# A hybrid decoder layer: order-only dependencies for the transfers of the first pair, and one mask with a difference of values

## The chip, the cores and the metric

The kernel runs on one core of a Trainium2 chip. The core has five engines that run side by side, each through its own instructions in order: TensorE (PE; its weight loads are listed as PEld), VectorE (DVE), ScalarE (ACT), GpSimd (POOL) and SyncE (SP). An instruction waits on semaphores where it needs another engine's result, and whatever stands behind it on its engine waits too. SP does no arithmetic here: it starts nearly all transfers between the chip's main memory and the on-chip memory, in the order of its queue. ACT and POOL start some as well. The metric is the device time of one execution in microseconds (us), lower is better. A profile is one execution recorded by the hardware profiler, and its own time stands beside the span from its first to its last instruction.

## The reference

The layer works on 2048 tokens of width 1024 in float32. In short:

```python
hn = rms_norm(h, mix_pre_g)
proj = hn @ w_in                       # q (8 heads of 64), k and v (2 heads), and the input of a GLU
s = q.k / 8 + bias[distance]           # each query sees itself and the 127 tokens before it
p = softmax over s and a learned sink per head
attn_out = p @ v
conv_out = silu(layer_norm(depthwise_conv31(glu) + b)) @ w_conv_pw
mixed = concatenate([attn_out, conv_out]) @ w_out
h = h + rms_norm(mixed, mix_post_g)
hn = rms_norm(h, ffn_pre_g)
ff = (silu(hn @ w_gate) * (hn @ w_up)) @ w_down      # inner width 2816
h = h + rms_norm(ff, ffn_post_g)
```

In the attention, queries are taken in blocks of 128. A block of queries sees the keys of its own block up to its own position, and those of the block before from the next position on. So for a query at place q and a key place k in the block, exactly one of the two keys counts: the current one for k <= q, the one before for k > q.

## The kernel before

The 2048 tokens are four tiles of 512 (t = 0 to 3), the feature dimensions blocks of 128. A matmul of float32 values is done as three matmuls of split values (a rounded high part, and the rest as low part), which is what `three` and `product` do; ACT makes the high parts and DVE or POOL the low parts (`split_w`, `split_f`, `lo`).

The stages have letters, which stand behind the @ in the names of the profile: A is the input projection (`stage_a`, one per tile), B the attention (`stage_b`), C the convolution, done as 31 multiply-adds per channel block on DVE (`stage_taps`, written to `y_scr`) and a tail (`stage_tail`), W the output projection with its norms (`stage_w`, `norm_w`), H the operands of the feed-forward part, F its first product with the gate and up weights, G its second with the down weights. F and G treat two tiles of tokens at once, the first pair (tiles 0 and 1, labels F0, G0) and the second (tiles 2 and 3, labels F2, G2), by Strassen's scheme with seven block products in place of eight. Some of the first products are made earlier (`stage_pre`), kept in `keeps` and loaded again (`fetch`) when the seven-product stage (`stage_p1`) needs them. `stage_p1` reads two tiles of weights per matrix (`loads`, lines 951 to 959), makes four sums of them on DVE (`sums`), splits them, multiplies, and stores the results in `mids`. `stage_tsums` (L1065) makes the sums of the down weights meanwhile and stores them in `td`. `stage_p2` loads blocks of `mids` (tiles `fa`) and of down weights or their sums (tiles `mb`) three steps ahead (`load`, L1117).

The order of the work is set by two things. The code runs one main stage and, beside it, several lanes (`Lane`), each of which is given turns by a hand-set rate: attention, convolution taps, convolution tails, output projections and operands of the feed-forward part are lanes. From that program order a scheduler makes the order of every engine's instructions with a timeline of its own: among the instructions that are ready on its timeline it takes the earliest in program order. An instruction can so be moved ahead of others that are not ready. `tied(r)` (L113) gives `r` an order-only dependency on the last matmul of the main stage, `lead_pe`: the scheduler does not place `r` before that matmul, but no semaphore and no wait on the chip comes from it. Before the change, `tied` is used for a few transfers (L1051, L1054, L1072). `defer(n, emit)` hands an instruction out n steps later in program order.

In the attention, `front(b)` makes the scores of a block of queries. The scores with the block before and with the current block are merged into one 128 x 128 square by the mask `upper` (L456), so only 128 columns go through the softmax. `back(b)` turns the probabilities on TensorE, ACT copies them out (L497), and POOL makes two masked copies of each group of four heads, one for the current block and one for the block before (L499). The matmuls (L517) add both products in one bank, with values from `vtok`, which holds the tile's four blocks of 128 tokens and the last block of the tile before (L414, L415). In the first block of all there is no block before.

The norms take a sum of squares of 1024 columns on ACT into a tile `junk` that nobody reads (L272, L738, L760).

The on-chip tiles come from rings with a tag and a fixed number of buffers, and a tile waits for the release of the one that had its buffer.

Of the kernel before, what the change touches and what calls it, by code (L numbers as in the profile page):

```python
# [23 lines left out]
D = 1024  # L24
# [13 lines left out]
def layer_kernel(ctx, tc, x, xT, cols, rows, sinks, relb, onehot, w_in, w_pw, w_out, w_gate, w_up, w_down, out):  # L38
# [28 lines left out]
    def sm(n, dt=F32):  # L67
        kind = "A" if lab[0][0] == "G" else lab[0][0]
        return sb.tile([P, 8], dt, tag="sm" + kind, name=nm("sm"), bufs=16)[:, 0:n]
# [49 lines left out]

    def defer(n, emit):  # L120
        later.append([n, emit])
# [91 lines left out]
    ones = cst.tile([P, 1], F32, name="ones")  # L213
# [19 lines left out]
    neg = cst.tile([P, 1], F32, name="neg")  # L233
# [8 lines left out]
    junk = cst.tile([P, D], BF16, name="junk")  # L242
    vtok = cst.tile([P, 5, P], F32, name="vtok")
# [83 lines left out]
    def stage_a(t, hn, before_kv, hooks, post=None):  # L327
# [79 lines left out]
        for i in range(4):  # L407
            oq = proj(10 + i)
            if i == 0:
                pv = mm()  # L410
                for s in range(4):
                    nc.tensor.transpose(pv[:, s * P : (s + 1) * P], vt[:, s * P : (s + 1) * P], ident)
                if t:
                    nc.vector.tensor_copy(vtok[:, 0], vtok[:, 4])  # L414
                nc.vector.tensor_copy(vtok[:, 1:5].rearrange("p a b -> p (a b)"), pv)  # L415
# [14 lines left out]
    def stage_b(t):  # L430
# [54 lines left out]
        def back(b):  # L485
# [3 lines left out]
            for g in range(2):  # L489
# [8 lines left out]
                for kb in range(1 if first else 0, 2):  # L498
                    nc.gpsimd.affine_select(  # L499
                        out=pg[:, kb].rearrange("p (i q) -> p i q", q=P),  # L500
                        in_=pg[:, 1].rearrange("p (i q) -> p i q", q=P),
                        compare_op=ALU.is_ge if kb else ALU.is_gt,
                        fill=0.0,
                        base=0,
                        pattern=[[0, 4], [1 if kb else -1, P]],
                        channel_multiplier=-1 if kb else 1,
                    )
# [51 lines left out]
    def stage_taps(t):  # L559
        L = f"C{t}"  # L560
        for c in range(4):
# [8 lines left out]
            nc.sync.dma_start(y_scr[c, :, t * T : (t + 1) * T], y)  # L570
# [62 lines left out]
    def stage_x():  # L633
        lab[0] = "X0"
        rel = cst.tile([32, 8], F32, name="rel")
# [96 lines left out]
    def norm_w(w, spill, acc, mtag):  # L732
# [3 lines left out]
        ssq = sm(4)  # L736
        for s in range(4):
            act(junk, acc[s], AF.Square, accum_out=ssq[:, s : s + 1])  # L738
            yield 0.5
            lab[0] = L  # L740
        r = rsqrt(ssq, 4, D, w < 3)
        yield 3
        lab[0] = L
        ssq2 = sm(4)
        for s in range(4):
# [14 lines left out]
            act(junk, acc[s], AF.Square, accum_out=ssq2[:, s : s + 1])  # L760
            yield 1.5
        lab[0] = L
        r2 = rsqrt(ssq2, 4, D, w < 3)
# [178 lines left out]
    def stage_p1(ws, ops, mid, keep):  # L942
# [8 lines left out]
        def loads(m):  # L951
            if m < len(MATS):
# [3 lines left out]
                nc.sync.dma_start(r0, src[2 * pr].rearrange("p (a b) -> p a b", a=2))  # L956
                r1 = t_("chl", (P, 2, T))
                nc.sync.dma_start(r1, src[2 * pr + 1].rearrange("p (a b) -> p a b", a=2))
# [38 lines left out]
        for q, (m, j, i, nst) in enumerate(todo):  # L997
# [10 lines left out]
            if j == 0:  # L1008
                bk = {}
                if not gate:  # L1010
                    blocks = {}
                    if pre:
                        blocks[3] = f2("fa")
                        nc.sync.dma_start(blocks[3], mid[0, pr])
# [17 lines left out]
            else:  # L1032
# [7 lines left out]
                else:  # L1040
# [3 lines left out]
                    if i in (3, 4, 6):  # L1044
# [20 lines left out]
    def stage_tsums(td):  # L1065
        L = "G0"
        for pr in range(NF // 2):
# [6 lines left out]
            b11, b12, b21, b22 = b  # L1074
            for to, o, p_, q_ in ((0, b11, b12, b11), (2, b12, b22, b12), (1, b22, b22, b11), (3, b21, b21, b22)):
                lab[0] = L
                vtt(o, p_, q_, ALU.subtract)
                nc.sync.dma_start(td[to, pr], o)
                yield 1

    def finish(L, gb, jobs, pool=True):
# [3 lines left out]
        for j, (rows_, halves) in enumerate(jobs):  # L1085
            for n in range(2):
                act(junk[:, 0:T], halves[n], AF.Square, scale=D**-0.5, accum_out=ssq[:, 2 * n + j : 2 * n + j + 1])
# [5 lines left out]
        for j, (rows_, halves) in enumerate(jobs):  # L1093
            ht = f4("wx" if L == "G0" else "mid")
            nc.sync.dma_start(ht, h_scr[rows_])
            for n in range(2):
                cs = slice(n * T, (n + 1) * T)
                stt(halves[n], halves[n], r[:, j : j + 1], ht[:, cs], ALU.mult, ALU.add)
                nc.sync.dma_start(out[rows_, cs], halves[n])
            yield 2.0  # L1100
            lab[0] = L

    def stage_p2(ws, am, td, last=False):
# [13 lines left out]
        def load(i):  # L1117
            if i < len(steps):
# [45 lines left out]
        def scale_even(h):  # L1164
            for b in (2 * h, 2 * h + 1):
                lab[0] = L
                c = home("c11", "x", b)
                act(junk[:, 0:T], c, AF.Square, scale=D**-0.5, accum_out=sse[:, b : b + 1])
# [69 lines left out]
        for b in range(4):  # L1238
# [4 lines left out]
            act(junk[:, 0:T], banks[b], AF.Square, scale=D**-0.5, accum_out=ssq)  # L1243
# [246 lines left out]
```

## Time and profile before

| what | value |
|---|---|
| time, median of 3 runs | 2036.23 us (2028.73 to 2038.02) |
| time of the profiled execution | 2033.91 us |
| its span | 2032.2 us |
| mean granted clock of TensorE | 0.987 |
| busy: TensorE, DVE, ACT, POOL | 1959.0, 1504.8, 988.8, 382.4 us |
| moved by transfers | 451.44 MB, 222 GB/s in the mean |
| attention masks on POOL (L499) | 62, from 129 to 592 us |
| seven-product stage of the first pair | about 686 to 1033 us |
| second product of the first pair | about 1033 to 1380 us |

In lines of the profile the form is "line engine operation out<-in", with the tile names of the program without numbers; a tile's letter behind the @ is its stage. `x62` counts instructions. In an answer about waits, "PE tr@B L108 <- POOL p@B L499: 10.4, 4, 6.8" says that TensorE stood idle before matmuls of L108 into tile `tr` of stage B, that the semaphore which came last was POOL's for L499, and that this took 10.4 us in 4 waits, the longest 6.8. In a timeline the first number is the start in us, the second the duration, and square brackets hold the idle time of the engine before it and what ended it. In rows of stretches "A:B length, ..." the busy times of PE, PEld, DVE, ACT and POOL follow with the number of instructions in brackets, then the granted clock of TensorE as a share of full speed, the share of time that the transfer engines were busy, and GB/s. Rows of one tile or line give the shortest, the median and the longest duration in ns.

### The profile page before, as it was taken

The numbers are of one execution on the slowest core, as the hardware profiler recorded it, in microseconds if no ns is written. First come the engines' busy times: TensorE is split into PE (matmuls) and PEld (weight loads), VectorE is DVE, ScalarE is ACT, GpSimd is POOL, SyncE is SP. The second block draws the span as 40 slices with busy tenths as digits, with TensorE's granted clock in tenths as the row PEclk, the third lists the DMA queues.
The fourth block names the chain that finished last, engine by engine and source line by source line (L and its number), as shares of the span: only waits on it lengthen the run. The fifth ranks groups of instructions, "written<-read, shape, count | busy, mean of one in ns | idle before, by whom it ended". The sixth has DMA issues, their size and how long they took to land. (4 is left out here: it accounts for less than half of the span.)

```text
span 2032.2 us, 27181 instructions
## 1 busy us (share of the span) xinstructions
PE 1959.0 (96%) x8826; PEld 1566.8 (77%) x8826; DVE 1504.8 (74%) x2664; ACT 988.8 (49%) x1938; POOL 382.4 (19%) x447
## 2 busy tenths in 40 slices
PE   8999999998889989999989999989999999999998
PEld 7877767776667778788878878878788888888886
DVE  5999887993895889888649985576756665545557
ACT  5455445456546633333346457556643433345443
POOL 6011224423111300000001012102523233221000
PEclk9999999999999999999999999999999999999999
DMA  8786645568558876777376778589944443266554
GB/s 310 268 290 234 207 129 187 189 221 276 184 174 305 291 236 235 271 248 255 133 265 208 231 251 297 188 285 335 335 154 161 150 171 115 98 228 230 193 187 165
DMA packets 234110, 451.44 MB, mean 222 GB/s; under 512 B 23496, under 2 KB 49264, under 8 KB 233968
## 3 DMA queue, kind: packets, MB, share of 16 engines
q1 hardware_dynamic: 211184, 411.96, 60.7%
q10 hardware_dynamic: 20544, 30.42, 4.1%
q0 software_dynamic: 2240, 7.34, 0.9%
q8 instruction: 69, 1.13, 0.2%
q14 instruction: 73, 0.60, 0.1%
HBM read 330.60 MB, written 119.02 MB: 221 GB/s over the span
## 5 line engine op out<-in xcount | busy, mean ns | idle before, releaser
L85 DVE SCALAR_TENSOR_TENSOR fc@C<-glu@C,colt,fc@C 128x512 f32<-128x512 f32 x480 | 371.7, 788 | 3.0
L108 PE MATMUL mm@F<-hl@H,w@F 128*128 128x512 f32 x1056 | 254.3, 392 | 3.1 <-ACT mm@F L909 3.1
L108 PE MATMUL mm@G<-hl@G,hl@G 128*128 128x512 f32 x924 | 229.1, 398 | 6.0 <-DVE x@G L85 5.3
L108 PEld LDWEIGHTS mm@F<-hl@H,w@F 128*128 128x128 f32 x1056 | 198.8, 189 | 45.6 <-ACT mm@F L909 4.0
L108 PEld LDWEIGHTS mm@G<-hl@G,hl@G 128*128 128x128 f32 x924 | 174.9, 192 | 43.9 <-ACT hl@G L782 5.9
L108 PE MATMUL mm@A<-hl@A,w@A 128*128 128x512 f32 x840 | 205.8, 396 | 2.3 <-DVE hl@A L85 1.2
L782 ACT ACTIVATE w@F<-chl@F 128x512 fp32r<-128x512 f32 x220 | 135.5, 625 | 145.3 <-PE mm@F L108 139.7
L108 PE MATMUL mm@G<-w@G,hl@G 128*128 128x512 f32 x876 | 199.5, 389 | 0.0
L108 PEld LDWEIGHTS mm@G<-w@G,hl@G 128*128 128x128 f32 x876 | 164.4, 188 | 34.1
L108 PEld LDWEIGHTS mm@A<-hl@A,w@A 128*128 128x128 f32 x840 | 154.9, 188 | 37.4 <-DVE hl@A L85 3.1
L85 DVE TENSOR_TENSOR w@F<-chl@F,w@F 128x512 fp32r<-128x512 f32 x198 | 146.6, 742 | 38.8 <-ACT w@F L782 38.2
L108 PE MATMUL mm@F<-mid@H,w@F 128*128 128x512 f32 x528 | 133.7, 398 | 4.7 <-ACT mm@F L909 3.4
L108 PE MATMUL mm@F<-p@H,w@F 128*128 128x512 f32 x528 | 130.8, 393 | 0.3 <-ACT at@F L1031 0.3
L108 PE MATMUL mm@F<-ql@H,w@F 128*128 128x512 f32 x528 | 127.4, 390 | 2.5 <-ACT w@F L782 2.2
L108 PE MATMUL mm@F<-x@H,w@F 128*128 128x512 f32 x528 | 125.8, 391 | 1.5 <-ACT fa@F L931 1.5
L108 PEld LDWEIGHTS mm@F<-mid@H,w@F 128*128 128x128 f32 x528 | 100.1, 191 | 27.6 <-ACT mm@F L909 4.0
L108 PEld LDWEIGHTS mm@F<-ql@H,w@F 128*128 128x128 f32 x528 | 98.9, 188 | 23.9 <-ACT w@F L782 2.8
L108 PEld LDWEIGHTS mm@F<-p@H,w@F 128*128 128x128 f32 x528 | 100.0, 190 | 22.0 <-ACT at@F L1031 1.1
L108 PEld LDWEIGHTS mm@F<-x@H,w@F 128*128 128x128 f32 x528 | 98.7, 188 | 22.7 <-ACT fa@F L931 1.9
L133 ACT ACTIVATE w@A<-raw@A 128x512 fp32r<-128x512 f32 x110 | 67.3, 626 | 88.4 <-PE mm@A L108 46.5
L108 PE MATMUL mm@W<-w@W,hl@W 128*128 128x512 f32 x384 | 100.4, 405 | 8.3 <-ACT hl@W L704 6.3
L108 PE MATMUL tr@W<-w@W,ql@W 128*128 128x512 f32 x384 | 98.8, 396 | 6.0 <-ACT mid@W L675 4.8
(299 smaller groups left out, 3368.3 us busy)
## 6 DMA issues: line engine op xcount, KB each, us to landing
mids<-fa@F SPq DMA_DIRECT2D x154, 256.0 KB, 2.6
raw@A<-w_in SPq DMA_DIRECT2D x55, 512.0 KB, 4.5
w@A<-lo_in SPq DMA_DIRECT2D x84, 256.0 KB, 3.5
fc@G<-mids SPq DMA_DIRECT2D x77, 256.0 KB, 3.4
fa@G<-mids SPq DMA_DIRECT2D x75, 256.0 KB, 4.4
gb@F<-keeps SPq DMA_DIRECT2D x72, 256.0 KB, 4.3
raw@W<-w_out SPq DMA_DIRECT2D x32, 512.0 KB, 5.4
w@W<-lo_out SPq DMA_DIRECT2D x48, 256.0 KB, 3.8
```

The source lines that it names most:

```text
L85: r = op(*args, **kw)
L108: r = nc.tensor.matmul(*args, **kw)
L133: act(w[:, 0], raw, AF.Copy)
L782: act(w[:, 0], x, AF.Copy)
```

## The change

It has these parts.

1. Attention: POOL makes one masked copy per group of heads, the one for the block before. The product with the current block takes the unmasked probabilities, and the product with the masked copy takes `vdif`, the values of the block before less those of the current block. This gives the same sum. `vdif` is made on DVE with subtractions after the copy of the values.
2. The first pair (`ws[0] == 0`): the weight loads, the loads of kept products and of a middle block in `stage_p1`, all loads of `stage_p2` and the final stores get an order-only dependency (`tie`). `loads` comes at the fourth step from the end of a matrix and not at the last, `fetch` at the third from the end and not the second. The stores of two middle blocks are deferred by a step and tied. The stores of `stage_tsums` are tied and go out one subtraction later. The final stores stand after the yield.
3. Both pairs: the store of the taps (`y_scr`) is tied.
4. Norms: `junk` has 512 columns, so the sums of squares in `norm_w` are made in halves and added (`squares`, `joined`); `row_norms` squares in place.
5. Small tiles: `ones` and `neg` share a tile, the bias table moves into a small ring, and the ring of label X is that of A.

```diff
+    def tie(on, r):
+        return tied(r) if on else r
...
+    def squares(row, to, s):
+        for n in range(2):
+            act(junk, row[:, n * T : (n + 1) * T], AF.Square, accum_out=to[:, 4 * n + s : 4 * n + s + 1])
+
+    def joined(s):
+        o = sm(4)
+        vtt(o, s[:, 0:4], s[:, 4:8], ALU.add)
+        return o
...
-    junk = cst.tile([P, D], BF16, name="junk")
-    vtok = cst.tile([P, 5, P], F32, name="vtok")
+    junk = cst.tile([P, T], BF16, name="junk")
+    vtok = cst.tile([P, 4, P], F32, name="vtok")
+    vdif = cst.tile([P, 4, P], F32, name="vdif")
...
-            act(junk, xt, AF.Square, accum_out=ssq[:, i : i + 1])
+            act(xt, xt, AF.Square, accum_out=ssq[:, i : i + 1])
...
                 if t:
-                    nc.vector.tensor_copy(vtok[:, 0], vtok[:, 4])
-                nc.vector.tensor_copy(vtok[:, 1:5].rearrange("p a b -> p (a b)"), pv)
+                    nc.vector.tensor_copy(vdif[:, 0], vtok[:, 3])
+                nc.vector.tensor_copy(vtok.rearrange("p a b -> p (a b)"), pv)
+                if t:
+                    vtt(vdif[:, 0], vdif[:, 0], vtok[:, 0], ALU.subtract)
+                vtt(vdif[:, 1:], vtok[:, 0:3], vtok[:, 1:], ALU.subtract)
...
-                for kb in range(1 if first else 0, 2):
+                if not first:
                     nc.gpsimd.affine_select(
-                        out=pg[:, kb].rearrange("p (i q) -> p i q", q=P),
+                        out=pg[:, 0].rearrange("p (i q) -> p i q", q=P),
                         in_=pg[:, 1].rearrange("p (i q) -> p i q", q=P),
...
-                    r = mat(o[sl], vtok[:, b + kb, sl], pt[g][:, kb], start=kb == 1, stop=first or kb == 0)
+                    r = mat(o[sl], vtok[:, b, sl] if kb else vdif[:, b, sl], pt[g][:, kb], start=kb == 1, stop=first or kb == 0)
...
-            nc.sync.dma_start(y_scr[c, :, t * T : (t + 1) * T], y)
+            tied(nc.sync.dma_start(y_scr[c, :, t * T : (t + 1) * T], y))
...
-            act(junk, acc[s], AF.Square, accum_out=ssq[:, s : s + 1])
+            squares(acc[s], ssq, s)
...
-                nc.sync.dma_start(r0, src[2 * pr].rearrange("p (a b) -> p a b", a=2))
+                tie(ws[0] == 0, nc.sync.dma_start(r0, src[2 * pr].rearrange("p (a b) -> p a b", a=2)))
...
-                nc.sync.dma_start(kept[m], keep[m])
+                tie(ws[0] == 0, nc.sync.dma_start(kept[m], keep[m]))
...
-                    if i in (3, 4, 6):
+                    if i in (3, 4) and ws[0] == 0:
+                        defer(1, lambda a=mid[{3: 0, 4: 4}[i], pr], s=s: tied(nc.sync.dma_start(a, s)))
+                    elif i in (3, 4, 6):
                         nc.sync.dma_start(mid[{3: 0, 4: 4, 6: 1}[i], pr], s)
...
             if j == nst - 4:
                 sums(m + 1)
-            if j == nst - 2:
+            if j == (nst - 1 if ws[0] else nst - 4):
+                loads(m + 2)
+            if j == (nst - 2 if ws[0] else nst - 3):
                 fetch(m + 1)
-            if j == nst - 1:
-                loads(m + 2)
...
                 vtt(o, p_, q_, ALU.subtract)
-                nc.sync.dma_start(td[to, pr], o)
+                if last:
+                    tied(nc.sync.dma_start(*last))
+                last = td[to, pr], o
                 yield 1
+            lab[0] = L
+            tied(nc.sync.dma_start(*last))
...
-                nc.sync.dma_start(rawa[i], am[ty, pr])
+                tie(not last, nc.sync.dma_start(rawa[i], am[ty, pr]))
...
-                        nc.sync.dma_start(rb[:, j], source(ty, pr + j))
+                        tie(not last, nc.sync.dma_start(rb[:, j], source(ty, pr + j)))
```

More of the change, by code (lines that the diff above doesn't have):

```diff
@@ L67, in sm @@
     def sm(n, dt=F32):
-        kind = "A" if lab[0][0] == "G" else lab[0][0]
+        kind = "A" if lab[0][0] in "GX" else lab[0][0]
         return sb.tile([P, 8], dt, tag="sm" + kind, name=nm("sm"), bufs=16)[:, 0:n]
@@ L212, in layer_kernel @@
         x0.append(xt)
-    ones = cst.tile([P, 1], F32, name="ones")
+    ones_neg = cst.tile([P, 2], F32, name="ones_neg")
+    ones, neg = ones_neg[:, 0:1], ones_neg[:, 1:2]
     nc.vector.memset(ones, 1.0)
@@ L634, in stage_x @@
         lab[0] = "X0"
-        rel = cst.tile([32, 8], F32, name="rel")
+        rel = sm(8)[0:32]
         nc.sync.dma_start(rel, relb)
@@ L759, in norm_w @@
             nc.sync.dma_start(h_scr[r0 : r0 + P], acc[s])
-            act(junk, acc[s], AF.Square, accum_out=ssq2[:, s : s + 1])
+            squares(acc[s], ssq2, s)
             yield 1.5
         lab[0] = L
-        r2 = rsqrt(ssq2, 4, D, w < 3)
+        r2 = rsqrt(joined(ssq2), 4, D, w < 3)
         yield 3
@@ L1013, in stage_p1 @@
                         blocks[3] = f2("fa")
-                        nc.sync.dma_start(blocks[3], mid[0, pr])
+                        tie(ws[0] == 0, nc.sync.dma_start(blocks[3], mid[0, pr]))
                 if pre:
@@ L1074, in stage_tsums @@
             b11, b12, b21, b22 = b
+            last = None
             for to, o, p_, q_ in ((0, b11, b12, b11), (2, b12, b22, b12), (1, b22, b22, b11), (3, b21, b21, b22)):
@@ L1086, in finish @@
             for n in range(2):
-                act(junk[:, 0:T], halves[n], AF.Square, scale=D**-0.5, accum_out=ssq[:, 2 * n + j : 2 * n + j + 1])
+                act(junk, halves[n], AF.Square, scale=D**-0.5, accum_out=ssq[:, 2 * n + j : 2 * n + j + 1])
                 vtt(halves[n], halves[n], gb[n], ALU.mult)
@@ L1098, in finish @@
                 stt(halves[n], halves[n], r[:, j : j + 1], ht[:, cs], ALU.mult, ALU.add)
-                nc.sync.dma_start(out[rows_, cs], halves[n])
             yield 2.0
             lab[0] = L
+            for n in range(2):
+                tie(L == "G0", nc.sync.dma_start(out[rows_, n * T : (n + 1) * T], halves[n]))
     def stage_p2(ws, am, td, last=False):
@@ L1167, in scale_even @@
                 c = home("c11", "x", b)
-                act(junk[:, 0:T], c, AF.Square, scale=D**-0.5, accum_out=sse[:, b : b + 1])
+                act(junk, c, AF.Square, scale=D**-0.5, accum_out=sse[:, b : b + 1])
                 ptt(c, c, gbs[0], ALU.mult)
@@ L1242, in stage_p2 @@
             ssq = sm(1)
-            act(junk[:, 0:T], banks[b], AF.Square, scale=D**-0.5, accum_out=ssq)
+            act(junk, banks[b], AF.Square, scale=D**-0.5, accum_out=ssq)
             g = f2("fa")
```

15 lines of the change are left out of this document (7 added, 8 removed).

## The prediction

> **What bounds the kernel now.** I read the busy times first, then TensorE's own waits, then the granted clock around the longest of them, and last the order of time around each.
>
> ```profile
> PE 1959.0 (96%) x8826; PEld 1566.8 (77%) x8826; DVE 1504.8 (74%) x2664; ACT 988.8 (49%) x1938; POOL 382.4 (19%) x447
> ...
> 1463.45 347.35 PE mm@F L108 x1524
> ```
>
> TensorE (PE) is busy for 96% of the span, and the stretch of the chain of work in the second line runs without a break: 347.35 us over 1524 matmuls is 0.228 us for one of 512 columns. The change removes no matmul, so all it can win is TensorE's idle time and what hangs on it. The waits of TensorE, and the clock after five of them (the column before the last two is the granted clock):
>
> ```profile
> PE tr@B L108 <- POOL p@B L499: 10.4, 4, 6.8
> PE mm@W L108 <- ACT hl@W L704: 6.3, 5, 3.0
> PE mm@G L108 <- DVE x@G L85: 5.3, 1, 5.3
> PE tr@W L108 <- ACT mid@W L675: 4.8, 1, 4.8
> PE mm@F L108 <- DVE gb@F L85: 3.9, 1, 3.9
> PE mm@F L108 <- ACT w@F L782: 2.2, 1, 2.2
> PE mm@F L108 <- ACT fa@F L931: 1.5, 1, 1.5
> PE mm@F L108 <- DVE w@F L85: 1.1, 1, 1.1
> ...
> 286.75:290.16 3.41, 3.41 (x19) 1.57 (x15) 3.37 (x3) 1.75 (x3) 2.16 (x2) 0.50 0.38 144
> 460.83:467.66 6.83, 3.92 (x10) 1.07 (x12) 3.50 (x5) 5.75 (x11) 4.13 (x5) 0.50 1.01 385
> 730.50:733.90 3.40, 3.40 (x9) 2.63 (x8) 3.40 (x7) 1.82 (x4) 0.00 (x0) 0.50 0.75 234
> 836.30:839.70 3.40, 3.40 (x10) 2.62 (x9) 3.40 (x7) 0.63 (x2) 0.00 (x0) 0.50 0.27 103
> 1194.70:1201.50 6.80, 5.60 (x15) 4.26 (x16) 6.80 (x11) 2.09 (x4) 0.00 (x0) 0.50 0.23 86
> ```
>
> The waits are few and long, and each of the longer ones is followed by a stretch of 3.4 or 6.8 us at half clock. A wait so costs its own length and half of the matmul time in that stretch: 1.7 us for 3.40 busy, 2.0 for 3.92. The shortest wait that I see followed by such a stretch is the one of 2.2 us at 835.5, below.
>
> **The masks.** The attention waits for POOL twice at length:
>
> ```profile
> 277.80 0.60 PE L496 MATMUL tr@B<-ident,p@B 128*128 128x128 f32 x4
> 283.43 0.57 ACT L497 ACTIVATE p@B<-tr@B 128x512 f32<-128x512 f32 x1
> 284.08 1.71 POOL L499 TENSOR_SCALAR_AFFINE_SELECT p@B<-p@B 128x512 f32<-128x512 f32 x2 [5.84 <-ACT p@B L497]
> 285.83 2.81 PE L108 MATMUL tr@B<-p@B,vtok 128*64 128x512 f32 x8 [3.08 <-POOL p@B L499]
> ...
> 456.19 7.50 POOL L499 TENSOR_SCALAR_AFFINE_SELECT p@B<-p@B 128x512 f32<-128x512 f32 x4 [5.45 <-ACT p@B L497]
> 456.75 1.29 DVE L85 TENSOR_TENSOR x@W<-fa@W,x@W 128x512 f32<-128x512 f32 x2
> 463.74 3.68 PE L108 MATMUL tr@B<-p@B,vtok 128*64 128x512 f32 x8 [6.77 <-POOL p@B L499]
> ...
> L499 POOL TENSOR_SCALAR_AFFINE_SELECT p@B<-p@B x62: 632/868/5287, 129.4 to 592.2; 128x512 f32<-128x512 f32 x62
> L415 DVE COPY vtok<-mm@A x4: 680/688/692, 82.5 to 468.6; 128x512 f32<-128x512 f32 x4
> L414 DVE COPY vtok<-vtok x3: 212/220/220, 90.9 to 386.4; 128x128 f32<-128x128 f32 x3
> ```
>
> 32 of the 62 selects go. The product with the current block then needs only the ACT copy (L497), and the one with the difference needs one select after it. In the instruction order of the two programs, 20 matmuls stood between the last transpose and the first product at 286 us, 31 stand there now; at 464 us it was 14 and is 25. Eleven matmuls are 2.5 us, a select 0.9. At 286 that covers the 3.1 us: with its slow stretch 3.1 + 1.7 = 4.8 us won. At 464 the four selects took 7.50 us, one of them 5.29, beside additions of two inputs on DVE. If that one stays and one of 0.64 follows, POOL is done at 456.2 + 5.9 = 462.1 instead of 463.7. TensorE has 2.5 us more to do from 457.0 and then the two unmasked products (0.9 together: half of the 3.68, at twice the clock), so it comes there at 460.4: 1.7 of 6.8 us stay, with no slow stretch, and 5.1 + 2.0 = 7.1 are won. Sum -11.9; bounds -1.9 (two selects at 0.9 and nothing else) and -13.6. GPSIMD Engine Reference, § 1. Specifications, of the Trainium skill has POOL's SBUF interfaces shared with VectorE, with contention against instructions with two SBUF inputs. The 5.29 us beside two-input additions agrees; without that rule both selects would take 0.64 and the sum would be 1.7 lower.
>
> The difference adds to DVE four subtractions of 128x384 (at most 0.69 each, by the copy of 128x512) and three of 128x128 (0.22): 3.4 us in all. They follow the copy of the values, and the next block of attention comes many matmuls later. That cover hides them: 0; if it is gone, +3.4. Merging `ones` and `neg`, the bias tile in a small ring, the `X` ring and the in-place square of the row norms move no work to another engine: 0.
>
> **The squares.** The last row is a tap of the convolution, for the chains below.
>
> ```profile
> L738 ACT ACTIVATE junk<-mid@W x12: 1041/1057/1060, 603.8 to 1318.8; 128x1024 bf16<-128x1024 f32 x12
> L738 ACT ACTIVATION_READ_ACCUMULATOR junk<-mid@W x12: 185/187/189, 604.8 to 1319.7; 128x1 f32 x12
> L1087 ACT ACTIVATE junk<-p@G x12: 613/620/635, 1365.9 to 2002.5; 128x512 bf16<-128x512 f32 x12
> ...
> L85 DVE SCALAR_TENSOR_TENSOR fc@C<-glu@C,colt,fc@C x480: 693/745/1890, 46.3 to 1187.9; 128x512 f32<-128x512 f32 x160
> ```
>
> 32 squares of 1024 columns become 64 of 512: each row of squares costs 2 x (0.62 + 0.19) - (1.06 + 0.19) = 0.37 us more, 1.5 for four, 11.8 in all on ACT, and eight small additions. ACT is 49% busy, which hides it except where a norm is waited for. One group is on the path by the slow stretch at 1194.7: +1.5, bounds 0 and +11.8.
>
> **Loads and stores of the first pair.** In the seven-product stage of the first pair (686 to 1033 us) the waits are these:
>
> ```profile
> 714.48 0.69 DVE L85 TENSOR_TENSOR chl@F<-chl@F 128x512 f32<-128x512 f32 x1 [3.88 <-DMA chl@F<-w_gate]
> 717.69 1.19 PE L108 MATMUL mm@F<-mid@H,w@F 128*128 128x512 f32 x4 [1.13 <-DVE w@F L85]
> 728.85 0.69 DVE L85 TENSOR_TENSOR wx@G<-wx@G 128x512 f32<-128x512 f32 x1 [2.54 <-DMA wx@G<-w_down]
> 730.19 2.26 PE L108 MATMUL mm@F<-yt@H,w@F 128*128 128x512 f32 x5 [3.89 <-DVE gb@F L85]
> 834.26 0.60 ACT L1017 ACTIVATE mm@F<-gb@F 128x512 f32<-128x512 f32 x1 [7.99 <-DMA gb@F<-keeps]
> 835.46 0.73 PE L108 MATMUL mm@F<-ql@H,w@F 128*128 128x512 f32 x2 [2.25 <-ACT w@F L782]
> ```
>
> Each has a transfer behind it that SP issued late, and an engine that waits for it in order with TensorE's operand queued behind. The tie is no wait on the chip: it fixes where SP's queue holds the transfer. So I counted in both programs, for each transfer, the matmuls between the last one that must be done before SP reaches it and the first that can't start until it has landed (its cushion). From about 717 us to the stage's end the transfers with under 50 matmuls (11 us) fall from 12 to 6, under 60 from 31 to 12, of some 210. The earlier weight loads gain most (gate: median 63 to 73, up: 75 to 84). The waits are worth 1.1 + 3.9 + 2.2 and two slow stretches of 1.7, 10.6 us; I take 9 of it, bounds 0 and -10.6. The stores of the middle values, put off by a step and behind its matmuls, free their buffers later by up to 2.7 us (12 matmuls); the in-place sums that need them come a step later still: 0. The four difference stores of `stage_tsums` go one step later, and the taps' and final stores (`y_scr`, `out`) behind a matmul; nothing reads them for a stage: 0.
>
> At the start of the second product the wait of 4.8 us has another such cause, the activations of the third output projection:
>
> ```profile
> 1046.55 0.63 ACT L704 ACTIVATE ql@W<-at@W 128x512 fp32r<-128x512 f32 x1 [5.14 <-DMA at@W<-mixT]
> 1047.72 2.77 PE L108 MATMUL tr@W<-w@W,ql@W 128*128 128x512 f32 x6 [4.76 <-ACT mid@W L675]
> ...
> at@W<-mixT SPq DMA_DIRECT2D x24, 256.0 KB, 4.6
> mb@G<-w_down SPq DMA_DIRECT2D x33, 256.0 KB, 4.2
> chl@F<-w_gate SPq DMA_DIRECT2D x22, 512.0 KB, 4.0
> ```
>
> That transfer's cushion goes from 39 matmuls to 77: -4.8 and, by the 1.7 of the other stretches, -6.5 in all; bounds 0 and -6.5.
>
> **What the new order costs.** At a few places the new program leaves TensorE next to nothing to do meanwhile, and there the chain of operations is a wait at least as long as itself. (1) First products, ahead of 686 us: one matmul after its last input TensorE needs a copy that ACT holds behind a split and three squares: 0.62 + 3 x 0.81 + 0.60 - 0.23 = 3.4, where 1.5 stands above (L931): +1.9, and 1.7 for a slow stretch. (2) Third step of the seven products: two additions, a tap and a split, 0.68 + 0.68 + 0.74 + 0.62 - 0.23 = 2.5, with 1.7. (3) Two later steps wait for DVE to empty a bank: 2 x (0.68 - 0.23) = 0.9. (4) Start of the second product: its first weights have 17 matmuls (3.9 us) for a transfer of 4.2 and a split and a subtraction of 0.6 each, 1.5, plus its queue: 2. (5) Where the attention of the fourth tile starts, the second projection's activations, which ACT splits ahead of a query's split, have 13 matmuls (3.0 us) for 4.6 + 0.6 + 0.6: 2.9, with 1.7. (6) The first projection's have 23 instead of 18: -1.1, from the 3.0 of the second wait line. Together +14.2; bounds 0 (the same engines are late anyway and the waits are spent elsewhere) and +20, with 1.7 more at the others.
>
> Sum: -11.9 + 1.5 - 9 - 6.5 + 14.2 = -11.7 against the profiled execution of 2033.9 (span 2032.2 and 1.7 around it), which lies 2.3 below the median of 2036.2 and inside the three runs: 2022.
>
> TensorE: Matmul & The Clock Gate, "Why this matters for your kernels", of the Trainium skill wants no idle gap over about 3 us, as one idle window of 3.4 us halves the clock. The wait of 2.25 us that stands above ahead of 836.3 at 0.50 disagrees, and the measurement decides. By that figure the stretches at (2) and (5) and the one at 836.3 would leave the sum, which would be 1.7 lower.
>
> **The rivals.** *The short chains cost nothing*, since TensorE arrives late at them: 2033.9 - 11.9 + 1.5 - 9 - 6.5 = 2008. For it: ACT is half idle. Against: each counts one to 25 matmuls. *The ties move waits and remove none*: both loads' gains are 0, 2033.9 - 11.9 + 1.5 + 14.2 = 2038, no change. For it: the transfers are the same and take 4 us, and every stall took another cause. Against: the counts. *Slower: the second product of the first pair starves.* Its 152 loads are tied too and come later: median cushion 95 to 80 for the left operand, 101 to 78 for the sums of weights; transfers of all kinds under 60 matmuls go from 22 to 44 between about 1027 and 1343 us. SP waits there for DVE to free a buffer, and the entries of projections stand in the same queue. One failure is the row x@G: 5.3 and a slow stretch of 2.8 (half of 5.60), 8 us. Three more make 2022 + 24 = 2046, slower by 0.5%; the second already brings no gain. Against: 60 matmuls are 13.7 us for some 6.
>
> **How the numbers follow.** A measurement of this kernel can tell about 0.5%, 10 us: faster is below 2026, slower above 2046. The forecast, 2012 to 2032, gets 0.46; no cost of the chains 0.22; ties without gain 0.19; starved loads 0.13. Faster: three quarters of the first and nearly all of the second, 0.56; slower 0.13 with a rest of the third, 0.14; the same 0.30. The range of 2000 to 2043 leaves out a part of the second and most of the last.
>
> **What would show it.** The page after should have 30 selects and no wait of `tr@B` for POOL over 2 us; no wait for `gb@F` or `w@F` of over 2 us between 700 and 1030 us, while ACT's wait for `keeps` shrinks; the wait for `mid@W` gone; new waits of 2 to 4 us at the places (1), (2) and (5). Wrong would make it waits for `hl@G` from 1050 to 1350 us, where TensorE is now full, or a mask that still takes 5 us at 464.

## The result and the profile after

The changed kernel takes 2046.64 us in the median (2045.15 to 2050.44), the kernel before 2035.66 beside it: a ratio of 1.0056, with a 95% interval of 1.0043 to 1.0069. The kernel before ran beside every set of runs below, and each ratio is to it; a difference between two ratios carries the uncertainty of both, 0.2 to 0.3%. I had forecast 2022 and a gain; it is 11 us slower. The profiled execution took 2045.81 us, 11.90 more than that of before.

First the busy times on the page of the changed kernel, then its waits of TensorE:

```profile
PE 1970.5 (96%) x8826; PEld 1567.6 (77%) x8826; DVE 1497.2 (73%) x2679; ACT 995.1 (49%) x2002; POOL 351.1 (17%) x415
```

```profile
PE mm@F L108 <- DVE gb@F L85: 5.4, 3, 3.4
PE tr@B L108 <- ACT ql@A L439: 4.5, 1, 4.5
...
PE mm@G L108 <- DVE hl@G L85: 4.0, 1, 4.0
PE mm@F L108 <- ACT fa@F L947: 3.3, 1, 3.3
PE mm@G L108 <- ACT hl@G L798: 3.3, 1, 3.3
PE mm@G L108 <- DVE x@G L85: 3.3, 1, 3.3
PE mm@G L108 <- ACT p@G L1177: 2.9, 1, 2.9
PE mm@F L108 <- ACT w@F L798: 2.8, 1, 2.8
...
PE mm@A L108 <- ACT w@A L136: 2.6, 1, 2.6
```

The work moved as the change says: POOL has 31 us less to do, ACT 6 more. The wait for POOL (10.4 us before) is no longer among the long ones, and that for ACT's `mid@W` is gone. In their places stand others of the same size, for ACT and DVE: TensorE's idle time, the span less its busy time, is 2032.2 - 1959.0 = 73.2 us before and 2044.1 - 1970.5 = 73.6 after. The stretches at half clock add up to 47.8 us before and 44.4 after, as far as the last matmul. So nearly the whole loss stands in TensorE's busy time, 11.5 us more for the same 8826 matmuls, and longer stretches of half clock do not explain it. How late TensorE is shows in the rows of two groups of matmuls, where the number ahead of "to" is the start of the first: before, and then after.

```profile
L108 PE MATMUL mm@F<-hl@H,w@F x1056: 387/389/628, 640.2 to 1802.3; 128*128 128x512 f32 x176
...
L108 PE MATMUL mm@G<-ql@G,hl@G x48: 388/389/389, 2008.3 to 2022.6; 128*128 128x512 f32 x48
```

```profile
L108 PE MATMUL mm@F<-hl@H,w@F x1056: 387/389/499, 651.2 to 1814.2; 128*128 128x512 f32 x176
...
L108 PE MATMUL mm@G<-ql@G,hl@G x48: 388/389/389, 2020.2 to 2034.5; 128*128 128x512 f32 x48
```

At 640 us, where the first products begin to use the second operand, the changed kernel is already 11.0 us late; at the last matmul it is 11.9. So nearly all of the loss is made ahead of that point, in the attention and the stages around it, though the masks are gone there. The rows of the stretches up to it, before and then after:

```profile
0.00:640.20 640.20, 609.03 (x2883) 458.21 (x2884) 529.14 (x1105) 330.78 (x754) 169.80 (x243) 0.99 0.68 226
```

```profile
0.00:651.20 651.20, 623.03 (x2882) 461.86 (x2883) 519.66 (x1116) 335.99 (x790) 143.37 (x211) 0.98 0.67 223
```

TensorE idles 31.2 us there before and 28.2 after: it waits 3.0 us less and is busy 14.0 us more. Stretches of half clock (17.1 us before, 23.9 after) explain some 3.4 of the 14.0. The rest is in the order of the matmuls. The attention's score matmuls load weights of 64 rows (64*128 in the profile, rows times columns), its products with the values weights of 64 columns (128*64), the projections 128*128. In the kernel before 13 score matmuls stand together; after, scores alternate with matmuls of a projection:

```profile
330.89 1.15 PE L108 MATMUL tr@B<-kz,ql@A 64*128 64x256 f32 x13
```

```profile
324.11 0.73 PE L108 MATMUL tr@B<-kz,ql@A 64*128 64x256 f32 x6
324.78 0.49 PE L108 MATMUL mm@A<-mid@A,w@A 128*128 128x512 f32 x1
325.20 0.39 PE L108 MATMUL tr@B<-kz,ql@A 64*128 64x256 f32 x2
325.52 0.50 PE L108 MATMUL mm@A<-mid@A,w@A 128*128 128x512 f32 x1
325.94 0.38 PE L108 MATMUL tr@B<-kz,ql@A 64*128 64x256 f32 x1
326.25 0.50 PE L108 MATMUL mm@A<-mid@A,w@A 128*128 128x512 f32 x1
...
329.21 1.65 PE L108 MATMUL mm@A<-mid@A,w@A 128*128 128x512 f32 x6
```

Thirteen scores and six matmuls of the projection take 5.1 us there (324.11 to 329.21), without a wait; the thirteen together take 1.15 and six of the projection in a row 1.4. Counted over the traces, TensorE goes 262 times from weights of one shape to weights of another up to this point before, and 330 times after. Taken from start to start at full clock, without idle time, these places take 12.1 us more in the changed kernel than in the one before, beyond what the same matmuls take among their like.

The longer waits have their part too, and two of them were forecast. Three from the timeline:

```profile
32.65 0.92 PE L108 MATMUL mm@A<-hl@A,w@A 128*128 128x512 f32 x2 [2.60 <-ACT w@A L136]
...
465.86 0.63 ACT L720 ACTIVATE hl@W<-at@W 128x512 fp32r<-128x512 f32 x1 [3.59 <-DMA at@W<-mixT]
466.39 0.58 ACT L439 ACTIVATE ql@A<-mm@A 128x512 fp32r<-128x512 f32 x1
467.03 0.80 PE L108 MATMUL tr@B<-kz,ql@A 64*128 64x256 f32 x4 [4.54 <-ACT ql@A L439]
...
634.17 1.06 ACT L947 ACTIVATE fa@F<-mm@F 128x512 f32<-128x512 f32 x2
634.80 1.65 PE L108 MATMUL mm@F<-x@H,w@F 128*128 128x512 f32 x3 [3.33 <-ACT fa@F L947]
```

The second and third are the chains (5) and (1) of the forecast. The first is none of them: the split of a weight on ACT comes after a copy and a tanh there, and ahead of them in the kernel before.

### The profile page after: what moved, and what is told of

Same layout as the page of the kernel before. It is cut to its first block, busy times and chain, and to the rows that moved or that the text cites. A ratio compares the mean times of both kernels' runs of the same rounds, so it can differ in the third digit from the quotient of the medians.

```text
span 2044.1 us, 27129 instructions
## 1 busy us (share of the span) xinstructions
PE 1970.5 (96%) x8826; PEld 1567.6 (77%) x8826; DVE 1497.2 (73%) x2679; ACT 995.1 (49%) x2002; POOL 351.1 (17%) x415
## 4 chain that ended last, share of the span: by engine, by line
PE 70%; DMA 12%; DVE 10%; issue 3%; ACT 3%; POOL 1%; SPq 1%; DVEq 0%; ACTq 0%; POOLq 0%
PE mm@F L108 31%; PE mm@G L108 15%; PE mm@A L108 12%; PE mm@W L108 4%; PE tr@B L108 3%; PE tr@W L108 2%; DVE fc@C L85 2%; DMA at@W<-mixT 2%; DVE w@F L85 1%; PE ct@C L108 1%; DMA chl@F<-w_up 1%; DVE mid@W L85 1%; DMA fc@G<-w_down 1%; DMA mb@G<-td 1%; DVE fa@F L85 1%
```

## The experiments

**The parts alone.** Theory A took from these rows that the attention part brings its own losses; rival B that the masks win and the ties lose; rival C that any edit makes the scheduler set another order, and that the order costs. The edits are those of the diff above, and for e3 and e4:

```diff
 e3:
-    ones = cst.tile([P, 1], F32, name="ones")
+    ones_neg = cst.tile([P, 2], F32, name="ones_neg")
...
-        rel = cst.tile([32, 8], F32, name="rel")
+        rel = sm(8)[0:32]
 e4, besides the mask and e3's edits:
-    junk = cst.tile([P, D], BF16, name="junk")
+    junk = cst.tile([P, D], I8, name="junk")
```

Expected of e1:

> The kernel before with the mask, the difference of values, the squares in halves and the shared small tiles, and with no transfer tied or moved. Theory A (the attention part brings its own losses: in the changed kernel's trace the work is 6 to 7 us late where the attention ends, at about 600 us, and loses 4 more at the first products at 631): about 2045 against 2036, 1.0045. Rival B (the masks win as forecast, the ties lose it): 2036 - 12 + 1.5 + the short chains (1) and (5), 8, = 2034 or less, 0.999 or below.

Expected of e2:

> The kernel before with the ties, the earlier loads and the later stores alone; masks, values and squares as before. Theory A: the rest of the changed kernel's loss, about +2, 2038, because the trace of the changed kernel loses 4 us from 651 to 1043 us and wins 3 back behind. Rival B: +10 or more, 2046 and above, with waits for hl@G or for transfers in the stages of the first pair that the kernel before does not have. My forecast's own terms would be 2036 - 9 - 6.5 + 5 = 2026.

Expected of e3:

> The kernel before with the three edits that move no work alone: the constants 1 and -1e30 in one tile, the bias tile in a ring of small tiles, that ring shared. Theories A and B: no change, 2036 within 3 us. Rival C (any edit makes the planner set another order, and the order alone is worth several us): away from 2036 by 4 us or more to either side, with other waits in other places, though no engine has other work to do.

Expected of e4:

> The kernel before with the mask, the difference of values and the shared small tiles; squares in one piece of 1024 columns as before, their unused output in one-byte numbers so that it takes no more room than in the changed kernel. Theory A: late by 6 where the attention ends and not at the first products: 2041, with a wait for the operand ql@A where the fourth tile's attention starts. My forecast for the masks alone: 2036 - 12 + 4.6 for chain (5) = 2028. Rival B: 2028 or less too, so a time above 2036 falls on A or on C.

| run | median, us | ratio to before | 95% interval |
|---|---|---|---|
| e1, attention part | 2040.62 | 1.0028 | 1.0013 to 1.0043 |
| e2, ties | 2040.95 | 1.0027 | 1.0012 to 1.0042 |
| e3, small tiles | 2039.94 | 1.0028 | 1.0014 to 1.0041 |
| e4, mask alone | 2047.48 | 1.0056 | 1.0034 to 1.0079 |

The result that counts is e3: it gives no engine other work, and costs as much as either real part. That is neither A nor B. What in its order costs the time stays open: its profiled execution is its fastest (2032.02 us). In its program 1.7% of TensorE's instructions follow another one than in the kernel before, and 11 to 12% of those of DVE, ACT and SP; in the changed kernel it is 12, 50, 40 and 48%.

**The order written out.** To hold the order fixed, every instruction was tied, without a semaphore, behind the one that stood ahead of it on its engine in a chosen program. e5 and e6 take the order of the kernel before, e7 gives the kernel before the order of e4.

```diff
+    for k in order_of:
+        i = blk[k]
+        e = str(i.engine)
+        if e in prev:
+            tc.add_manual_dep(i, prev[e].name, mybir.DependencyInfo(mybir.DependencyClass.NoSync, ...), reason="order")
+        prev[e] = i
```

Expected of e5:

> e3's three edits again (constants in one tile, the bias tile in a shared ring), but with the order of the kernel before written out: every instruction of the five engines is tied behind the one that stood ahead of it in the kernel before. Rival C (the order alone cost e3 its 0.28%): back to the kernel before, 1.000 within 0.001. If the edits themselves cost (a wait for a buffer in the shared ring, the constants' tile), it stays at 1.003.

Expected of e6:

> e4's mask and difference of values with the order of the kernel before written out in the same way; only the selects that go and the subtractions that come are free. By my forecast's working the mask alone wins in that order too, less where the products now stand closer: at 286 us 20 matmuls (4.5 us) stand for a copy of 0.6, the stall of 4.8 goes; at 464 us 14 matmuls (3.2 us), of 6.8 some 3 stay: -8 in all, 2026 beside 2034, 0.996. Theory A (the mask part itself loses): 1.003 or more.

Expected of e7:

> The counterpart: the work of the kernel before (both masks, no difference of values) in e4's order, written out. Rival C: the order is what costs, so it is as slow as e4 or slower, since the masks' stalls come back: 1.006 to 1.010. Theory A: the order is harmless, 1.000.

| run | work | order | ratio to before | 95% interval |
|---|---|---|---|---|
| e5 | before, small tiles | before | 0.9992 | 0.9978 to 1.0006 |
| e6 | one mask, small tiles | before | 0.9960 | 0.9944 to 0.9977 |
| e4 | one mask, small tiles | new | 1.0056 | 1.0034 to 1.0079 |
| e7 | before | new | 1.0117 | 1.0094 to 1.0140 |

This settles A against C: the order costs, and the mask wins. With the order held, the mask wins: 0.32% (6.5 us) from e5 to e6, and 0.61% (12.4 us) from e7 to e4. With the work held, the order that came with it costs 0.96% (19.5 us) from e6 to e4 and 1.17% (23.8 us) from the kernel before to e7. About half of that is TensorE's changes between shapes of weights: up to the first products there are 262 in e5 and e6 as in the kernel before, and 338 in e4 and e7, where they take 11 to 12 us more. The traces agree on the mask: POOL's selects keep TensorE waiting 11.0 us in e7 and 0.4 in e4. (e4 and e6 hold the unused `junk` as one-byte numbers; a square takes 1.06 us either way.) e6, at 2027.27 us, beats both kernels. Its own row shows the price left at the fourth tile's masks, 6.8 us before:

```profile
452.59 5.01 POOL L621 TENSOR_SCALAR_AFFINE_SELECT p@B<-p@B 128x512 f32<-128x512 f32 x2 [6.30 <-ACT p@B L619]
...
457.65 0.65 PE L226 MATMUL tr@B<-p@B,vdif 128*64 128x512 f32 x2 [3.28 <-POOL p@B L621]
```

**The squares, and the two transfer stages one by one.** e8 adds the squares in halves to e6; their second halves stand right behind the first, and the 12 row norms in place are left to the scheduler. e9 and e10 tie the loads of one stage each and leave the rest of TensorE's order as it was. The other engines' order is not held in e9 and e10: 13 and 14% of DVE's instructions follow another one than in the kernel before, so these two runs measure the ties together with the order that came with them.

```diff
 e9:
+                tie(ws[0] == 0, nc.sync.dma_start(r0, src[2 * pr].rearrange("p (a b) -> p a b", a=2)))
...
+            if j == (nst - 1 if ws[0] else nst - 4):
+                loads(m + 2)
 e10:
+                tie(not last, nc.sync.dma_start(rawa[i], am[ty, pr]))
...
+                        tie(not last, nc.sync.dma_start(rb[:, j], source(ty, pr + j)))
```

Expected of e8:

> The whole attention part (e1: mask, difference, squares in halves, shared small tiles) with the order of the kernel before written out, second halves and sums of squares set right behind. If the order is what e1 lost, this is e6's gain and the squares' term: 1.5 us above e6 by my working (bounds 0 and +11.8), so 2029, 0.997. If the squares cost on their own, it is 1.000 or more.

Expected of e9:

> The kernel before with the ties, the earlier loads and the put-off stores of the first pair's seven-product stage alone. TensorE's order is that of the kernel before up to the 3000th matmul and from the 4500th on, so a difference belongs to this stage (about 700 to 1030 us). My forecast: -9 for the loads, +4.2 for chain (2), +0.9 for (3): 4 us faster, 0.998. By the changed kernel's trace, which loses 4 us there: 1.002.

Expected of e10:

> The kernel before with the ties of the second product's loads alone, so that TensorE's order differs only between the 4000th and the 6500th matmul (about 930 to 1490 us). My forecast: -6.5 for the wait for mid@W at 1047 and +2 for chain (4): 0.998. My slower rival (the stage starves): 8 us for each new wait, three of them 1.012. Rival C, the planner's other order in 2500 matmuls with its own waits: 1.002 to 1.006 without starved loads, that is with waits for engines and not for transfers.

e8 gave 0.9996 (0.9980 to 1.0012), 0.36% or 7.3 us above e6; e9 1.0011 (0.9997 to 1.0025); e10 0.9993 (0.9980 to 1.0006). Neither e9 nor e10 can be told from the kernel before. All three miss my terms to the slow side. The timeline of e8, with the old order throughout, at the norm ahead of the first products:

```profile
608.84 0.17 DVE L293 TENSOR_TENSOR sm@W<-sm@W 128x4 f32<-128x4 f32 x1 [2.16 <-ACT junk L289]
...
622.97 0.63 ACT L289 ACTIVATE junk<-mid@W 128x512 bf16<-128x512 f32 x1 [2.79 <-DVE mid@W L203]
...
625.43 0.80 PE L226 MATMUL mm@F<-x@H,w@F 128*128 128x512 f32 x1 [3.20 <-ACT fa@F L1062]
```

and the same matmuls in e6:

```profile
619.36 2.81 PE L226 MATMUL mm@F<-x@H,w@F 128*128 128x512 f32 x11 [1.22 <-ACT fa@F L1053]
```

DVE stands 2.16 us until the last half is squared, then adds the halves; the rows that it scales come later, ACT stands 2.79 us for the first of them, and the copy for TensorE is queued behind its squares: 3.20 us where e6 has 1.22. So at this place the squares cost by a chain through several engines, not by ACT's time alone. It is 2 us of the 7.3; where the rest lies, and what the free row norms have in it, stays open.

In e9 the waits at 717, 730 and 835 us are gone, as forecast. Two come instead, at the third step of the seven products and 190 us later:

```profile
712.04 0.78 PE L108 MATMUL mm@F<-mid@H,w@F 128*128 128x512 f32 x2 [2.76 <-ACT w@F L785]
...
914.61 0.69 DVE L85 TENSOR_TENSOR wx@G<-fc@G,wx@G 128x512 f32<-128x512 f32 x1 [1.39 <-DMA fc@G<-w_down]
...
921.23 0.68 DVE L85 TENSOR_TENSOR gb@F<-gb@F,mm@F 128x512 f32<-128x512 f32 x1
...
921.97 1.65 PE L108 MATMUL mm@F<-yt@H,w@F 128*128 128x512 f32 x3 [3.94 <-DVE gb@F L85]
```

The second is the wait that stood at 730, 3.89 us for `gb@F` behind a `w_down` transfer: DVE waits 1.39 us for a transfer of the difference stage and then works off its operations without a pause, and the one that TensorE needs is the last of eleven. So the late transfer has 1.39 us of the 3.94, and DVE's queue the rest. In e10 the wait for `mid@W` is gone too, and again two stand in its place:

```profile
1033.18 0.63 ACT L785 ACTIVATE hl@G<-mb@G 128x512 fp32r<-128x512 f32 x1 [2.37 <-DMA mb@G<-w_down]
...
1034.38 2.93 PE L108 MATMUL mm@G<-hl@G,hl@G 128*128 128x512 f32 x6 [3.80 <-ACT hl@G L785]
...
1197.46 0.69 DVE L85 TENSOR_TENSOR mid@W<-at@W,mid@W 128x512 f32<-128x512 f32 x1 [4.19 <-DMA at@W<-x]
...
1200.74 0.69 DVE L85 TENSOR_TENSOR mid@W<-at@W,mid@W 128x512 f32<-128x512 f32 x1 [2.59 <-DMA at@W<-x]
...
1201.53 1.06 ACT L763 ACTIVATE junk<-mid@W 128x1024 bf16<-128x1024 f32 x1 [4.72 <-DVE mid@W L85]
...
1204.25 2.08 PE L108 MATMUL mm@G<-hl@G,hl@G 128*128 128x512 f32 x4 [6.22 <-ACT hl@G L785]
```

The first is chain (4), twice my 2 us. In the second DVE waits for two loads of the residual rows (`x`), ACT for the row of the norm that DVE makes of them, and the splits that TensorE needs are queued behind ACT's square. So both waits go back in part to transfers that land late, as the slower rival had it, but two such waits do not make this run slower than the kernel before: the wait for `x@G` is 3.1 us here and 5.3 there, and that of 2.6 for `ct@C` is gone.

**The changed kernel with a part of the old order.** e11 holds the old order up to the first products that use the second operand (640 us) and leaves the rest to the scheduler, ties and all. e12 is the same without the squares in halves. e13 and e14 hold it to 96 and 290 us only.

Expected of e11:

> The changed kernel with everything it changes, but with the order of the kernel before written out as far as the first products of the first pair (about 640 us); from there on the planner's own order. If the parts add up, e8's -0.04% and e2's +0.27%: 1.002, 2040 beside 2035. If the order of the first 640 us is not what costs, it stays at the changed kernel's 1.0056.

Expected of e12:

> The same without the squares in halves: the mask and the difference in the old order as far as 640 us, and behind it all the ties, with e2's order on TensorE. Parts that add up give e6's -0.40% and e2's +0.27%: 0.9987. If the ties win once nothing else is moved, as my forecast had it, below e6: 0.993.

Expected of e13:

> The changed kernel with the old order written out only as far as the second tile's projections (about 96 us), the planner's order from there on. The changed kernel is 3.2 us late at that point, e11 1.5. If the loss of 16 us against e11 lies in many places, this wins back only the 2 to 3 us of the first tile: 1.0045. If the start sets all that follows, it falls to e11's 0.998.

Expected of e14:

> The same with the old order as far as the fourth tile's projections (about 290 us), so that the attention of the last tiles and the output projections of the first pair (place (5) at 462 us, place (1) at 631 us) are still the planner's. Many places: 4 us better than the changed kernel, 1.0036, and the rest of the loss against e11 lies between 290 and 640 us. One early place: 0.998 as well.

| run | old order up to | ratio to before | 95% interval |
|---|---|---|---|
| changed kernel | - | 1.0056 | 1.0043 to 1.0069 |
| e13 | 96 us | 1.0053 | 1.0040 to 1.0067 |
| e14 | 290 us | 1.0011 | 0.9996 to 1.0025 |
| e11 | 640 us | 0.9979 | 0.9966 to 0.9993 |
| e12, without the squares | 640 us | 0.9969 | 0.9953 to 0.9984 |

The same edits are 0.21% faster with the old order of the first 640 us, and 0.56% slower with the new one: 0.77%, 15.7 us, is the price of that order. It lies in many places: holding the first tile's order wins nothing to speak of (against the 2 to 3 us that I expected), the next two tiles' 0.42%, the stretch from 290 to 640 us 0.32%. The changes between shapes of weights up to the first products go the same way. Their time stands beside that of the kernel before, counted in one trace of each run:

| run | changes of shape | their time against before |
|---|---|---|
| before, e2, e8, e11, e12 | 262 | -0.7 to +0.2 us |
| e14 | 302 | +7.5 us |
| e13 | 337 | +10.6 us |
| e1, changed kernel | 330 | +11.8, +12.1 us |

So most of the 15.7 us is this. Which waits make up the rest I did not separate, since the scheduler's order after the held part changes too. The row of e11 that answers to the two above (its line numbers are shifted by the table of the order):

```profile
L159 PE MATMUL mm@F<-hl@H,w@F x1056: 387/389/628, 644.5 to 1803.3; 128*128 128x512 f32 x176
```

4.3 us late there, where the changed kernel is 11.0. One execution is no median, though: e3's profiled one took 2032.02 us and its median is 2039.94. So the ratios carry the sums here, and single rows only the places.

## Why the prediction was wrong

The step that failed is the one under all others. By the prediction's own steps:

- **What bounds the kernel**: this step failed. It took a matmul's time as fixed ("0.228 us for one of 512 columns") and concluded that all the change can win is TensorE's idle time and what hangs on it. So no term of the sum stands for the order of the matmuls themselves, which the change also sets anew. What the runs showed in its place: idle time stayed (73.2 and 73.6 us), the stretches of half clock are together 3.4 us shorter, and busy time grew by 11.5, for which the changes between shapes of weights account, with 12.1 us more up to the first products. That it is the order and not the edits is shown by e5 to e7 and e11. That it is the shapes rests on the counts and starts in the traces, which part the runs of the old order from those of the new; no run changes the shapes' order alone.
- **The masks, -11.9**: right for the work. -12.4 us in the new order (e7 to e4), -6.5 in the old (e5 to e6), where fewer matmuls cover them and 3.28 of 6.77 us stay. But the cover that I counted, matmuls of other stages between transposes and products, has its own price: it is some of these changes of shape.
- **The squares, +1.5**: mis-sized, as far as e6 to e8 show it, where they cost 7.3 us; from e12 to e11 it is 2.0, which can't be told from 0 or from 1.5. The upper bound of 11.8 held. I counted ACT's time alone; the wait of the first products grew by 2 us through engines waiting for each other in the norm. And the slow stretch at 1194.7, by which I put one group on the path, follows a wait for a transfer of the taps; the wait of 5.3 us for `x@G`, to which I gave the same stretch, ends at 1350:

```profile
1195.18 1.09 PE L554 MATMUL ct@C<-ident,fc@C 128*128 128x128 f32 x4 [2.56 <-DMA fc@C<-y_scr]
...
1349.99 2.47 PE L108 MATMUL mm@G<-hl@G,hl@G 128*128 128x512 f32 x5 [5.32 <-DVE x@G L85]
```

- **Loads of the seven-product stage, -9** with +5.1 for chains (2) and (3): measured +2.2 (e9, -0.6 to +5.1), with the other engines' order free. The three waits went, and (2) came as forecast, 2.76 us for 2.5. But (3) was put at 0.45 us a time, a bank emptied, and is 3.94 where the `w_down` transfer is late again and DVE's queue is long. In this run the wait that comes from DVE's order was not removed by the earlier loads; it showed up where the next such transfer was late.
- **The second product's wait for `mid@W`, -6.5** with +2 for chain (4): measured -1.4 (e10, -4.1 to +1.2), with 3.80 for (4) and 6.22 behind the norm.
- **"What the new order costs", +14.2**: this step rests on the first and failed with it. It priced the new order by waits alone, and the sign went wrong. Of it 3.6 for (1), 4.6 for (5) and -1.1 for (6), 7.1 in all, belong to the first 640 us; the order there costs 15.7 (changed kernel to e11). (1) and (5) are there, at 3.33 and 4.54 us with stretches of half clock of 6.8 and 10.2 us, not 3.4; (6) came out, with 1.84 us for 3.0. Yet all waits up to there are together 3.0 us shorter than before. The rest I could not see by counting matmuls between two instructions, for I never asked which matmuls they were. I had also put the small tiles, the shared ring and the row norms at 0 because they move no work: the first two alone (e3) cost 0.28%, and e5 shows that none of it is work.
- **The rivals.** The time of the slower one, 2046, came out by luck: it had the loss in the second product, and behind 651 us the changed kernel loses only 0.9 us. Its mechanism shows in e10, where two late loads reach TensorE, without a loss that can be measured. "The ties move waits and remove none" fits e9 and e10, and I gave it too little; with the other engines' order held it was not run. That an order kept from the kernel before is worth about 1% over what the scheduler sets anew was in no rival, and neither was a price for the order of TensorE's own matmuls.

The Trainium skill's "TensorE: Matmul & The Clock Gate", section "Why this matters for your kernels", has idle gaps of more than about 3 us bring the half clock. The wait of 2.60 us ahead of 32.65, with a stretch of half clock from 33.0 to 36.4, disagrees again; the measurement decides:

```profile
33.00:36.40 3.40, 2.97 (x8) 1.91 (x7) 0.40 (x1) 1.82 (x4) 3.40 (x4) 0.50 0.06 22
```

## What to carry to other kernels

Where a scheduler sets the order, an edit's price is that of its work plus that of the new order, and the second can be the larger: hold the old order while the work is measured, and change the order as an edit of its own. Split TensorE's loss into idle time, half clock and busy time before looking for waits: when the same matmuls are busy for longer, look at which stand side by side. A stall that comes from an engine's order, with one late input ahead of many operations, need not be gone when its transfer is moved; look for where the next late input will stand. Count what the small edits do to the order before putting them at nothing.

## What the runs showed of the hardware

The price of a change between shapes of weights, from the start of a matmul to that of the next, at full clock and as the median over ten traces: a matmul of 512 columns with weights 128*128 takes 0.227 us ahead of its like and 0.319 ahead of a score matmul (64*128). One with weights 128*64 takes 0.522 us ahead of one with 128*128; among their like these take 0.226 in the mean. Why, the traces do not show.

The stretches of half clock lie on a fixed grid. In the changed kernel's execution all ten start on it, among them those at 33.0, 340.2, 466.5, 633.8, 719.1 and 1043.4 us, which is 90, 127, 176, 201 and 296 times 3.413 us after the first. In the kernel before, those at 460.83, 730.5, 836.3 and 1194.7 us lie 51, 130, 161 and 266 times 3.413 us after that at 286.75. Two waits of the same kind, in stretches cut on that grid (PE's busy time stands first, the granted clock third from the end):

```profile
712.26:715.68 3.42, 1.94 (x9) 1.29 (x7) 1.38 (x3) 0.00 (x0) 0.00 (x0) 1.00 0.98 353
715.68:719.09 3.41, 1.05 (x3) 0.59 (x4) 3.41 (x6) 2.17 (x4) 0.00 (x0) 1.00 1.02 379
719.09:722.50 3.41, 3.41 (x9) 2.63 (x8) 3.41 (x7) 1.88 (x4) 0.00 (x0) 0.50 1.00 377
923.91:927.32 3.41, 1.87 (x9) 1.21 (x7) 2.96 (x6) 0.63 (x1) 0.00 (x0) 1.00 0.90 311
927.32:930.73 3.41, 1.60 (x7) 1.34 (x8) 3.41 (x6) 1.39 (x3) 0.00 (x0) 1.00 0.95 365
930.73:934.15 3.42, 3.42 (x17) 2.81 (x16) 3.42 (x7) 1.50 (x3) 0.00 (x0) 1.00 0.40 117
```

A wait of 2.76 us (at 717) with a shorter one behind it leaves 1.05 us busy in one cell of the grid, and the next cell runs at half clock. A longer wait, 3.35 us ahead of 929, is cut in two by the grid, leaves 1.87 and 1.60 us, and costs only itself. But busy time in a cell is not the whole rule. In this execution every cell at full clock with up to 1.3 us busy was followed by half clock (the first, in which the program starts, aside), and none from 1.6 on; in between both occur (1.57 us at 336.8 was followed by it, 1.58 at 592.8 was not). And in e6 a cell with 1.96 us was followed by half clock:

```profile
564.00:567.40 3.40, 1.96 (x18) 1.42 (x17) 0.38 (x2) 0.76 (x2) 0.00 (x0) 1.00 0.91 248
567.40:570.80 3.40, 3.40 (x8) 2.57 (x9) 3.33 (x6) 1.41 (x3) 1.06 (x1) 0.50 0.67 227
```

So the 1.7 us that I added to each wait of 2.2 and more depends on where the wait falls on the grid, and near the limit on more than that.
